# Two accumulating transfers behind a pair's q and k reads, and later starts for the heads of a gated linear attention, in a one-core encoder layer

## The chip, the cores and the metric

The kernel runs on one core of a Trainium2 chip and computes one layer of an encoder in one launch. The metric is the device time of one execution in microseconds; the time of a kernel is the median of its timed runs. Lower is better.

The core has a matmul engine (PE, whose weight loads the profile lists apart as PEld), a vector engine (DVE), a scalar engine (ACT), a general engine (POOL) and a queue engine (SP). PE reads the on-chip memory SBUF and writes eight banks of the accumulator memory PSUM, each 128 partitions by 512 float32. SP and POOL start the transfers (DMA) that carry data between the large off-chip memory and SBUF; POOL can also start a transfer that adds what it carries to what lies at its destination.

## What is computed

The layer normalizes x (512 rows of 2048), projects it once with a wide matrix, gives half of the projected columns to an attention with three dilations and the other half to a gated linear attention, joins both, projects back, and ends with a gated feed-forward block. Cut to what matters here:

```python
def reference(x, ...):
    h = rmsnorm(x, attn_norm_w[l])
    proj = h @ w_in[l]
    aq, ak, av, gq, gk, gv, gr, glr = jnp.split(proj, split_idx, axis=-1)
    attn = mixture_of_dilations(_heads(aq, 16), _heads(ak, 16), _heads(av, 16), rel_bias_table)
    ...
    # gated linear attention, 4 heads, both directions
    fwd = gla_causal(qh, kh, vh, log_a_f)
    bwd = flip(gla_causal(flip(qh), flip(kh), flip(vh), flip(log_a_b)))
    o = fwd + bwd
    o = o * lax.rsqrt(jnp.mean(o * o, axis=-1, keepdims=True) + NORM_EPS)
    gla_out = (_merge_heads(o) * gla_norm_w[l]) * jax.nn.silu(gr)
    mixed = jnp.concatenate([attn_out, gla_out], axis=-1) @ w_out[l]
    x = x + mixed
    h = rmsnorm(x, ffn_norm_w[l])
    x = x + (silu(h @ w_gate[l]) * (h @ w_up[l])) @ w_down[l]
    return rmsnorm(x, final_norm_w)
```

## The kernel before

**Products.** Every float32 operand is split into a high part and a low part of PE's rounded float32 type, and a product is three matmuls: high by high, high by low, low by high. ACT makes the high part (a cast) and DVE the low part (the difference). The matmuls of the plain projections are L346, L347 and L348. One such matmul starts 0.23 us after the one before; I call these the job matmuls.

**Order of the work.** The program is written as Python generators. A main line runs through the projections (jobs) and between two products lets side work go one step on: `run_side` takes a step of the generators in `side` (attention, linear attention), and `urgent` holds generators that go first. What an engine executes is fixed by the order in which these steps emit instructions; each engine works its own list in order, and an instruction that waits holds up all that stand behind it on that engine.

**The last unit of the front.** `Front.run` computes 16 units of the projection with seven products in place of eight (a Strassen-like scheme). Unit u leaves its result in a buffer `c_` by `evac7`: ACT and DVE combine seven PSUM banks, and then POOL starts four accumulating transfers (L1640 to L1643) that add three more buffers (r1, r2, r3) to `c_`. `finish` multiplies `c_` by the rows' scale (DVE, L1743) and POOL writes it to off-chip memory (L1744); for units 8 to 15 the destination is `qkd`, the attention's q and k. Of the last unit, u = 15, the multiplication and the write are kept back in `fr.late`, which `before_first` calls at step 8 of the next job (the projection of gv).

**Reads of a pair.** Attention works on pairs of heads. `read_qk` starts eight POOL reads for each pair (L574, 128 KB each, `a<-qkd`), and `load_qk` turns them into operands: four ACT instructions (L598) and four DVE instructions (L594). ACT L704 and DVE L710 make the high and low part of an attention unit's transposed weights; PE L696 is the transpose ahead of them.

**POOL's transfers.** A transfer that POOL starts reports its end on one of eight semaphores, taken in turn (in the rows below DMASW0 to DMASW7). A POOL transfer waits until the one that stands eight transfers ahead of it has landed.

**Linear attention.** `gla(h)` is a generator for one head, some 25 steps long. In its order: two PSUM banks z with the gate's projection (PE L977); ACT and DVE turn them into running sums and exponentials (`centre`, `exps`, `times`); then, for each direction d, a bank `tr` with transposes of k (PE L1071) and a bank `a` with k times q (PE L1074), which DVE copies under a mask into a zeroed buffer T (L1077) while ACT copies `tr`; then sums over blocks (PE L1096), states and outputs, the norm, and at the end two banks of transposes (PE L1166) that DVE scales and gates (L1169). `heads` then makes high and low parts of the result (ACT L963, DVE L956), which the output projection uses as stationary or moving operand. T is zeroed by POOL (L1066), and for every second head POOL also starts the reads of v (L906).

`turns` runs the four heads staggered: it lets at most two heads go on by one step each in a round, and starts a new head every `APART` = 12 rounds. PSUM banks are handed out from a list of free ones, the one that has been free longest first, so the order in which the steps ask decides which bank a step gets, and whose release it must wait for.

Of the kernel before, what the change touches and what calls it, by code (L numbers as in the profile page):

```python
# [29 lines left out]
NG = 4  # L30
# [82 lines left out]
def put(*slots):  # L113
    for s in slots:
        if s.home is not None:
            s.home.free.append(s.i)


def layer(nc, tc, x, attn_norm_w, w_in, rel_table, gw_f, gb_f, gw_b, gb_b, gla_norm_w, w_out,
# [7 lines left out]
    with tc.manual_schedule(), \  # L127
# [677 lines left out]
                yield  # L805
            urgent.append(last_pair(NH // 2 - 1))

        def turns(todo, apart):

            now, n = deque(), 0  # L810
            while todo or now:
                if n % apart == 0 and todo:
                    now.append(todo.popleft())
                for _ in range(2):
                    if _ < len(now):
                        g = now[0]
                        now.rotate(-1)
                        if next(g, 0) == 0:
                            now.remove(g)
                            continue  # L820
                    yield
                n += 1
# [85 lines left out]
        def evac_gv(pr):  # L908
            def f(banks):
                for t in range(4):  # L910
                    if t % 2 == 0:
                        v = s4.get(F32, [P, 2, 512])
                    if t % 2:
                        dve.tensor_scalar(v.t[:, 1], banks[t].t, rstd1[:, t:t + 1], None, op0=OP.mult)
                    else:
                        act.activation(v.t[:, 0], banks[t].t, AF.Copy, scale=rstd1[:, t:t + 1])
                    put(banks[t])
                    if t % 2:
                        pool.dma_start(out=gvd[2 * pr + t // 2], in_=v.t.rearrange("p b c -> p (b c)"))
                        put(v)  # L920
                if pr == 0:
                    side.append(silus())
                    side.append(turns(deque(gla(h) for h in range(NG)), APART))
            return f

        grd = dr.tile([4, P, 1024], F32, name="grd")
# [40 lines left out]
        def gla(h):  # L967
# [82 lines left out]
            exps(1)  # L1050
            yield
            times(1)
            if h % 2 == 0:
                load_gv(h // 2)
            yield
# [4 lines left out]
            if h == NG - 1:  # L1060
                put(*G["res"])

            T, kt = [], []
            for d in range(2):
                T.append(s2.get())
                pool.memset(T[d].t, 0.0)  # L1066
            for d in range(2):
                tr, a = ps.get(), ps.get()
                for b in range(4):
# [203 lines left out]
        def before_first(i):  # L1273
            if i == 1:
                urgent.appendleft(load_qk(0))
            if i == 4:
                load_v(0)
            if i == 8:
                fr.late()

        n_front = len(jobs)
        RATES = (4.5, 4.0)
        APART = 12
        for pr in range(2):
            j = job("B", [piece512(w_in, C_GV + pr * 512, k) for k in range(0, KT, 2)], list(range(KT)), acts_h,
                    evac_gv(pr), rate=RATES[0], start=None if pr else gstart, limit=3,
# [222 lines left out]

        class Feed(Blocks):  # L1510

# [96 lines left out]
            def evac7(self, u, banks):  # L1611


                a, z = slice(0, 256), slice(256, 512)
                add = lambda o, x_, y_: dve.tensor_tensor(o, x_, y_, op=OP.add)  # L1615
                sub = lambda o, x_, y_: dve.tensor_tensor(o, x_, y_, op=OP.subtract)
                c_ = s4.get(F32, [P, 2, 512])
                c = c_.t.rearrange("p f t -> p (f t)")
                m1, t2, t1, t3, m2, t4, b22 = (b.t for b in banks)
                t, v, r1, r2, r3 = (s2.get() for _ in range(5))  # L1620
                act.copy(t.t[:, a], m1[:, a])
                act.copy(r3.t[:, a], t1[:, z])
                act.copy(r2.t[:, z], t1[:, z])
                act.copy(r3.t[:, z], t3[:, z])
                act.copy(r1.t[:, a], m2[:, z])
                act.copy(c[:, 512:768], t4[:, a])
                act.copy(r2.t[:, a], t4[:, z])
                act.copy(c[:, 256:512], b22[:, a])
                act.copy(r1.t[:, z], b22[:, z])
                add(t.t[:, a], t.t[:, a], m1[:, z])  # L1630
                sub(t.t[:, z], t.t[:, a], t2[:, a])
                sub(t.t[:, z], t.t[:, z], t2[:, z])
                add(v.t[:, a], t1[:, a], t.t[:, z])
                add(v.t[:, z], t3[:, a], t.t[:, z])
                add(c[:, 768:1024], t1[:, a], v.t[:, z])
                add(c[:, a], m2[:, a], t.t[:, a])
                put(*banks)
                yield
                add(c[:, 256:768], c[:, 256:768], v.t)
                pool.dma_start(out=c[:, 0:512], in_=r1.t, accum_op=OP.add)  # L1640
                pool.dma_start(out=c[:, 512:1024], in_=r2.t, accum_op=OP.add)
                pool.dma_start(out=c[:, 256:768], in_=r3.t, accum_op=OP.add)
                pool.dma_start(out=c[:, 768:1024], in_=r3.t[:, z], accum_op=OP.add)  # L1643
                put(r1, r3, t, r2, v)
                for _ in range(3 if u < len(self.units) - 2 else 7):
                    yield
                yield from self.finish(u, c_, c)
# [73 lines left out]

        class Front(Feed):


            def __init__(self):
                self.units = [(w_in, C_GR + g * 256) for g in range(4)] + [(w_in, C_GQ), (w_in, C_GK)] + \
# [26 lines left out]
            def run(self):  # L1753
                banks = {}
                for i, (u, q) in enumerate(self.seq):
                    banks.setdefault(u, [])
                    self.load()
                    self.split(i)
                    self.sums(i + 1)
                    self.sums(i + 2)  # L1760
                    self.split(i + 1)
                    if u == len(self.units) - 1 and q < 3:
                        st.until, st.limit = in_pieces, q + 1
                        st.load()
                    while 2 * q + 1 not in xi:
                        run_side(1)
                    if u == len(self.units) - 1 and q == 3:
                        st.split(jobs[n_front].first + 2)
                    self.products(i, banks[u])
                    if u == len(self.units) - 1:  # L1770
                        for p in (2 * q, 2 * q + 1):
                            put(*xi.pop(p)["slots"])
                        if q == 1:
                            for _ in read_qk(0):
                                pass
                        if q == 2:
                            gla_operands()
                    done = None
                    if q == self.per - 1:
                        if u == len(self.units) - 1:  # L1780
                            s2.free.rotate(14)
                        done = self.evac7(u, banks.pop(u))
                        next(done)
                        if u == len(self.units) - 1:
                            next(done)
                    run_urgent()
                    if done:
                        urgent.append(done)

        fr = Front()  # L1790
# [469 lines left out]
```

## Time and profile before

| | us |
|---|---|
| median of 3 timed runs | 2164.08 (2163.97 to 2167.96) |
| the profiled execution, its own time | 2162.85 |
| span of the profiled execution | 2161.1 |
| PE busy in it | 2145.8 |
| DVE busy | 1851.8 |
| ACT busy | 1226.6 |
| POOL busy | 381.9 |

PE is busy in all but 15.3 us of the span. The time outside the span (2162.85 less 2161.1) is 1.75 us. In the profile a row of the timeline gives the start, the duration, the engine, the line, the operation, output and inputs by their names in the program, and in brackets how long the engine had been idle and what ended that. Matmuls overlap: one lasts about 0.4 us while the next starts after 0.23 us, so a loss on PE is read from start to start.

### The profile page before, as it was taken

The numbers are of one execution on the slowest core, as the hardware profiler recorded it, in microseconds if no ns is written. First come the engines' busy times: TensorE is split into PE (matmuls) and PEld (weight loads), VectorE is DVE, ScalarE is ACT, GpSimd is POOL, SyncE is SP. The second block draws the span as 40 slices with busy tenths as digits, with TensorE's granted clock in tenths as the row PEclk, the third lists the DMA queues.
The fourth block names the chain that finished last, engine by engine and source line by source line (L and its number), as shares of the span: only waits on it lengthen the run. The fifth ranks groups of instructions, "written<-read, shape, count | busy, mean of one in ns | idle before, by whom it ended". The sixth has DMA issues, their size and how long they took to land.

```text
span 2161.1 us, 35266 instructions
## 1 busy us (share of the span) xinstructions
PE 2145.8 (99%) x12754; PEld 1896.5 (88%) x12754; DVE 1851.8 (86%) x3153; ACT 1226.6 (57%) x2236; POOL 381.9 (18%) x531
## 2 busy tenths in 40 slices
PE   9999999999999999999999999999999999999998
PEld 7888888888888889888888888888888899999987
DVE  5699999878877778899899998998989888888795
ACT  7455555478876446455555555555555655555462
POOL 0011222232222010021122121221122120021300
PEclk9999999999999999999999999999999999999999
DMA  6377777877586763567677667776776985576982
GB/s 203 124 186 184 182 178 185 198 215 219 176 244 196 254 235 100 153 173 185 179 178 197 172 185 187 180 185 176 185 191 173 265 211 177 178 183 155 281 310 78
DMA packets 268220, 411.53 MB, mean 190 GB/s; under 512 B 19725, under 2 KB 164349, under 8 KB 268046
## 3 DMA queue, kind: packets, MB, share of 16 engines
q1 hardware_dynamic: 206110, 274.59, 40.1%
q0 software_dynamic: 61616, 134.15, 28.4%
q8 instruction: 101, 1.65, 0.3%
q14 instruction: 73, 0.60, 0.1%
q10 hardware_dynamic: 320, 0.53, 0.1%
HBM read 289.57 MB, written 66.42 MB: 165 GB/s over the span
## 4 chain that ended last, share of the span: by engine, by line
PE 90%; DVE 4%; DMA 4%; ACT 1%; issue 1%; POOL 0%; DVEq 0%; SPq 0%; ACTq 0%; POOLq 0%
PE ps L1595 31%; PE ps L1581 16%; PE ps L346 6%; PE ps L347 6%; PE ps L348 6%; PE ps L1962 5%; PE ps L1961 5%; PE ps L1960 5%; DMA b<-a 3%; PE ps L696 1%; DVE b L1504 1%; DMA a<-qkd 1%; PE ps L2155 1%; PE ps L2157 1%; PE ps L2156 1%
## 5 line engine op out<-in xcount | busy, mean ns | idle before, releaser
L1499 ACT CAST b<-b 128x1024 fp32r<-128x1024 f32 (+1 forms) x601 | 549.0, 944 | 405.6 <-DVE b L1504 209.7
L1504 DVE TENSOR_TENSOR b<-b,b 128x1024 fp32r<-128x1024 f32 (+1 forms) x601 | 630.6, 1084 | 31.7 <-ACT b L1499 20.2
L1595 PE MATMUL ps<-b,b 128*128 128x512 f32 x1760 | 517.2, 393 | 0.4 <-ACT b L1499 0.2
L1595 PE MATMUL ps<-a,b 128*128 128x512 f32 x1488 | 436.4, 393 | 0.2 <-DVE b L1615 0.2
L1595 PEld LDWEIGHTS ps<-b,b 128*128 128x128 f32 x1760 | 298.1, 188 | 33.2 <-ACT b L1499 0.7
L1581 PEld LDWEIGHTS ps<-b,b 128*128 128x128 f32 x1760 | 289.8, 190 | 42.6 <-DVE b L1504 0.3
L1581 PE MATMUL ps<-b,b 128*128 128x256 f32 x1760 | 318.1, 280 | 0.0
L1581 PEld LDWEIGHTS ps<-a,b 128*128 128x128 f32 x1488 | 246.5, 189 | 39.9 <-DVE b L1504 1.2
L1595 PEld LDWEIGHTS ps<-a,b 128*128 128x128 f32 x1488 | 248.9, 188 | 25.3 <-issue 0.4
L1581 PE MATMUL ps<-a,b 128*128 128x256 f32 x1488 | 267.6, 281 | 0.4 <-DVE b L1504 0.4
L1486 DVE TENSOR_TENSOR b<-b 128x512 f32<-128x512 f32 x276 | 189.2, 685 | 22.3 <-PE ps L1962 12.2
L1960 PE MATMUL ps<-b,b 128*128 128x256 f32 x624 | 176.6, 283 | 0.0
L1961 PE MATMUL ps<-b,b 128*128 128x256 f32 x624 | 176.6, 283 | 0.0
L1962 PE MATMUL ps<-b,b 128*128 128x256 f32 x624 | 176.6, 283 | 0.0
L346 PE MATMUL ps<-b,b 128*128 128x512 f32 x336 | 136.5, 406 | 0.2 <-DVE b L477 0.2
L348 PE MATMUL ps<-b,b 128*128 128x512 f32 x336 | 131.9, 392 | 0.0
L347 PE MATMUL ps<-b,b 128*128 128x512 f32 x336 | 131.8, 392 | 0.0
L1488 DVE TENSOR_TENSOR b<-b,b 128x256 f32<-128x256 f32 x276 | 117.5, 426 | 9.5
L1487 DVE TENSOR_TENSOR b<-b,b 128x256 f32<-128x256 f32 x276 | 117.3, 425 | 9.6
L1640 POOL DMA_DIRECT2D b<-a x58 | 50.2, 866 | 414.9 <-ACT b L1499 266.5
L1960 PEld LDWEIGHTS ps<-b,b 128*128 128x128 f32 x624 | 119.8, 192 | 0.0
L1961 PEld LDWEIGHTS ps<-b,b 128*128 128x128 f32 x624 | 119.8, 192 | 0.0
(296 smaller groups left out, 3972.8 us busy)
## 6 DMA issues: line engine op xcount, KB each, us to landing
b<-in_w_gate_dram SPq DMA_DIRECT2D x109, 512.0 KB, 4.0
b<-in_w_in_dram SPq DMA_DIRECT2D x94, 512.0 KB, 4.0
b<-in_w_up_dram SPq DMA_DIRECT2D x88, 512.0 KB, 4.2
b<-in_w_down_dram SPq DMA_DIRECT2D x88, 512.0 KB, 5.2
b<-a POOLq DMA_DIRECT2D x174, 256.0 KB, 4.6
b<-in_w_out_dram SPq DMA_DIRECT2D x32, 512.0 KB, 5.7
gd<-b POOLq DMA_DIRECT2D x22, 512.0 KB, 3.9
b<-gd SPq DMA_DIRECT2D x22, 512.0 KB, 7.7
```

Source lines behind the costliest of these rows:

```text
L346: mm(o, xh.t[:, c], wh.t[:, w], start=first and not on, stop=False, skip_group_check=on)
L347: mm(o, xh.t[:, c], wl.t[:, w], start=False, stop=False, skip_group_check=on)
L348: mm(o, xl.t[:, c], wh.t[:, w], start=False, stop=last, skip_group_check=on)
L1486: dve.tensor_tensor(s_[:, :, 0:2], r[:, :, 1:3], r[:, :, 0:1].to_broadcast(shape), op=OP.add)
L1488: dve.tensor_tensor(s_[:, :, 3], s_[:, :, 2], r[:, :, 3], op=OP.add)
L1499: act.copy(o, src)
L1504: dve.tensor_tensor(o, src, h, op=OP.subtract)
L1581: mm(o, wl, xh, start=False, stop=end, skip_group_check=True)
L1595: mm(o.rearrange("p (s t) -> p s t", s=2), wh, x_, start=first and p == 0, stop=False, skip_group_check=True)
L1960: mm(o, xh[:, t], wh, start=first and h == 0, stop=False, skip_group_check=True)
L1961: mm(o, xh[:, t], wl, start=False, stop=False, skip_group_check=True)
L1962: mm(o, xl[:, t], wh, start=False, stop=last, skip_group_check=True)
```

## The change

Three things are changed.

The last unit of the front is `parted`: after the first two accumulating transfers its generator stops, and the second two (L1642, L1643; in the new file L1651, L1652) are started by `before_first` at step 6 of the gv job. What is left of the generator is kept in `fr.rest`, not in `urgent`. Buffers t and v are given back before the stop.

`turns` starts the heads at rounds 0, 13, 25 and 37, in place of 0, 12, 24 and 36.

The two T buffers of a head are taken and zeroed two steps earlier, ahead of the reads of v.

```diff
-        def turns(todo, apart):
+        def turns(todo, starts):
 
             now, n = deque(), 0
             while todo or now:
-                if n % apart == 0 and todo:
+                if n in starts and todo:
                     now.append(todo.popleft())
...
             times(1)
+            T = [s2.get() for _ in range(2)]
+            for d in range(2):
+                pool.memset(T[d].t, 0.0)
             if h % 2 == 0:
                 load_gv(h // 2)
             yield
...
-            T, kt = [], []
-            for d in range(2):
-                T.append(s2.get())
-                pool.memset(T[d].t, 0.0)
+            kt = []
...
             if i == 4:
                 load_v(0)
+            if i == 6:
+                next(fr.rest)
             if i == 8:
+                for _ in fr.rest:
+                    pass
                 fr.late()
...
-        APART = 12
+        STARTS = (0, 13, 25, 37)
...
         class Feed(Blocks):
+            parted = False
...
                 pool.dma_start(out=c[:, 0:512], in_=r1.t, accum_op=OP.add)
                 pool.dma_start(out=c[:, 512:1024], in_=r2.t, accum_op=OP.add)
+                if self.parted and u == len(self.units) - 1:
+                    put(t, v)
+                    yield
+                    t = v = None
                 pool.dma_start(out=c[:, 256:768], in_=r3.t, accum_op=OP.add)
                 pool.dma_start(out=c[:, 768:1024], in_=r3.t[:, z], accum_op=OP.add)
-                put(r1, r3, t, r2, v)
+                put(*(o for o in (r1, r3, t, r2, v) if o))
...
         class Front(Feed):
+            parted = True
...
                     run_urgent()
-                    if done:
+                    if done and u == len(self.units) - 1:
+                        self.rest = done
+                    elif done:
                         urgent.append(done)
```

On POOL, at the end of the front, the rows before were these. `b_499` is the last unit's `c_`, `b_478` that of the unit before; the reads into `a_` are the second pair's, and the names in brackets are the semaphores that a row waits for (DMASW0 to 7 are the eight of POOL's own transfers, DMAHW those of transfers that SP starts).

```order
L1640 DMA b_499_4315<-a_142_4318 128x512 [waits DMASW3_49,DVE_49,Activation_49]
L1641 DMA b_499_4315<-a_143_4319 128x512 [waits DMASW4_49]
L1642 DMA b_499_4315<-a_144_4320 128x512 [waits DMASW5_49,DMASW4_49,DMASW3_49]
L1643 DMA b_499_4315<-a_144_4320 128x256 [waits DMASW6_49]
L1744 DMA qkd<-b_478_4107 128x1024 [waits DMASW7_49,DVE_49]
L574 DMA a_160_4466<-qkd 64x512 [waits DMASW0_49]
L574 DMA a_160_4466<-qkd 64x512 [waits DMASW1_49]
L574 DMA a_162_4468<-qkd 64x512 [waits DMASW2_49,PE_49]
L574 DMA a_162_4468<-qkd 64x512
L574 DMA a_161_4467<-qkd 64x512 [waits DMAHW0_49]
L574 DMA a_161_4467<-qkd 64x512 [waits DMASW5_49]
L574 DMA a_163_4469<-qkd 64x512 [waits DMASW6_49,PE_49]
```

The rows now:

```order
L1645 DMA b_499_4315<-a_142_4318 128x512 [waits DMASW3_49,DVE_49,Activation_49]
L1646 DMA b_499_4315<-a_143_4319 128x512 [waits DMASW4_49]
L1754 DMA qkd<-b_478_4107 128x1024 [waits DMASW5_49,DVE_49]
L574 DMA a_158_4463<-qkd 64x512 [waits DMASW6_49]
L574 DMA a_158_4463<-qkd 64x512 [waits DMASW7_49]
L574 DMA a_160_4465<-qkd 64x512 [waits DMASW0_49]
L574 DMA a_160_4465<-qkd 64x512 [waits DMASW1_49]
L574 DMA a_159_4464<-qkd 64x512 [waits DMASW2_49]
L574 DMA a_159_4464<-qkd 64x512 [waits DMASW3_49]
L574 DMA a_161_4466<-qkd 64x512 [waits DMAHW0_49,DMASW4_49]
L574 DMA a_161_4466<-qkd 64x512 [waits DMASW5_49]
L1651 DMA b_499_4315<-a_144_4320 128x512 [waits DMASW6_49]
```

The write of `b_478` and the eight reads now stand right behind the first two accumulating transfers. The old L1642 waits for both of these to land (DMASW3 and DMASW4), since it adds to the same buffer; now the sixth read waits for DMASW3 and the seventh for DMASW4, and the second two accumulating transfers come after the eighth.

On PE, where the first head of the linear attention makes its banks `tr` (L1071) and `a` (L1074) and the second head its two banks z (L977), the rows before were these; the digit behind `ps` is the PSUM bank, and the other rows are job matmuls.

```order
L1071 MATMUL ps1_324_6866<-idn_71,a28_381_6770 128x128 x4
L1074 MATMUL ps3_325_6867<-a13_380_6769,a28_381_6770 128x128 x4
L346 MATMUL ps6_321_6743<-b9_643_6686,b27_590_5987 128x512
L347 MATMUL ps6_321_6743<-b9_643_6686,b27_590_5987 128x512
L348 MATMUL ps6_321_6743<-b9_643_6686,b27_590_5987 128x512
L977 MATMUL ps2_326_6883<-a9_157_4452,a14_358_6372 128x512
L977 MATMUL ps4_327_6885<-a9_157_4452,a2_362_6436 128x512
L346 MATMUL ps7_322_6744<-b9_643_6686,b27_590_5987 128x512
L347 MATMUL ps7_322_6744<-b9_643_6686,b27_590_5987 128x512
L348 MATMUL ps7_322_6744<-b9_643_6686,b27_590_5987 128x512
L1071 MATMUL ps3_328_6893<-idn_71,a32_385_6803 128x128 x4
L1074 MATMUL ps1_329_6894<-a17_384_6802,a32_385_6803 128x128 x4
```

The same place now, from behind the first two rows, which are as before (`tr` of the first direction in bank 1, `a` in bank 3):

```order
L346 MATMUL ps7_322_6743<-b9_644_6685,b27_591_5986 128x512
L347 MATMUL ps7_322_6743<-b9_644_6685,b27_591_5986 128x512
L348 MATMUL ps7_322_6743<-b9_644_6685,b27_591_5986 128x512
L1071 MATMUL ps2_326_6884<-idn_71,a10_383_6802 128x128 x4
L1074 MATMUL ps4_327_6885<-a32_382_6801,a10_383_6802 128x128 x4
L346 MATMUL ps0_323_6744<-b9_644_6685,b27_591_5986 128x512
L347 MATMUL ps0_323_6744<-b9_644_6685,b27_591_5986 128x512
L348 MATMUL ps0_323_6744<-b9_644_6685,b27_591_5986 128x512
L977 MATMUL ps3_328_6902<-a9_157_4450,a15_356_6371 128x512
L977 MATMUL ps1_329_6904<-a9_157_4450,a2_360_6435 128x512
```

Before, the second direction's `tr` took bank 3, which the first direction's `a` had held. Now it takes bank 2 and its `a` bank 4, and the second head's z take banks 3 and 1, six job matmuls later than before.

At the end of the last head, on DVE, the rows before were these; `b29` and `b2` are the operands that `heads` makes (L956), and L1555 and L218 are other work of the weights to come and of the output projection.

```order
L1169 SCALAR_TENSOR_TENSOR a10_482_7915<-ps6_384_7910,wcol_74,b30_605_6240 128x512
L1169 SCALAR_TENSOR_TENSOR a18_483_7922<-ps4_385_7917,wcol_74,b30_605_6240 128x512
L1555 TENSOR_TENSOR b19_715_7850<-b19_715_7850 128x2x128 x2
L218 TENSOR_TENSOR a33_481_7901<-b24_709_7765,a20_480_7900 128x512
L1555 TENSOR_TENSOR b22_716_7890<-b22_716_7890 128x2x128
L956 TENSOR_TENSOR b29_720_7939<-a10_482_7915,b29_720_7939 128x512
L1555 TENSOR_TENSOR b22_716_7890<-b22_716_7890 128x2x128
L956 TENSOR_TENSOR b2_722_7949<-a18_483_7922,b2_722_7949 128x512
```

And now (L1560 is the old L1555):

```order
L1169 SCALAR_TENSOR_TENSOR a12_478_7921<-ps5_384_7916,wcol_74,b12_606_6239 128x512
L1169 SCALAR_TENSOR_TENSOR a2_479_7928<-ps6_385_7923,wcol_74,b12_606_6239 128x512
L218 TENSOR_TENSOR a14_477_7899<-b24_710_7754,a29_476_7898 128x512
L1560 TENSOR_TENSOR b11_718_7880<-b11_718_7880 128x2x128 x3
L956 TENSOR_TENSOR b23_723_7948<-a12_478_7921,b23_723_7948 128x512
L218 TENSOR_TENSOR a10_481_7932<-b24_710_7754,a32_480_7931 128x512
L956 TENSOR_TENSOR b19_724_7955<-a2_479_7928,b19_724_7955 128x512
```

About as much DVE work stands between L1169 and L956 as before, while on PE 12 job matmuls now stand between L1166 and the first use of the result, where 18 stood.

More of the change, by code (lines that the diff above doesn't have):

```diff
@@ L922, in f @@
                     side.append(silus())
-                    side.append(turns(deque(gla(h) for h in range(NG)), APART))
+                    side.append(turns(deque(gla(h) for h in range(NG)), STARTS))
             return f
```

## The prediction, made before the changed kernel had run

> **What bounds the kernel now.** I read the page's busy times first.
>
> ```profile
> span 2161.1 us, 35266 instructions
> PE 2145.8 (99%) x12754; PEld 1896.5 (88%) x12754; DVE 1851.8 (86%) x3153; ACT 1226.6 (57%) x2236; POOL 381.9 (18%) x531
> ```
>
> PE sets the end: 15.3 us of the span are not PE's. The change removes no matmul, so it can win only where PE stands idle. The view of busy time by windows says where that is (start and end, length, PE busy with its count, granted clock, DMA share, GB/s):
>
> ```profile
> 430.00:460.00 30.00, 28.49 (x145) 1.00 0.84 257
> 460.00:610.00 150.00, 149.10 (x878) 1.00 0.64 193
> 635.00:660.00 25.00, 23.42 (x117) 1.00 0.71 222
> 660.00:700.00 40.00, 39.75 (x202) 1.00 0.67 212
> ```
>
> Most of the rest lies in the kernel's last stage, which no edit touches. The edits reach 430 to 460 (1.51 us idle), 460 to 610 (0.90), 635 to 660 (1.58) and 660 to 700 (0.25): 4.24 us in all is the most that could go. The view of PE's waits names the two large ones (who waits <- for whom: us, times, longest):
>
> ```profile
> PE ps L1071 <- DVE a L1077: 1.6, 1, 1.6
> PE ps L696 <- DVE b L710: 1.5, 1, 1.5
> ```
>
> Each is one wait. They are the two places that the change aims at.
>
> **The first stall, at 447.55.** The chain of waits followed back from it (start, duration, what):
>
> ```profile
> 424.32 11.39 DMA b<-a
> ...
> 438.42 8.43 DMA a<-qkd
> ...
> 448.59 0.70 DVE b L710
> ```
>
> POOL stood before L1642 (its row below) until the second accumulating transfer (L1641, started at 424.32) had landed at 435.71; behind it stood the write of the unit before and all eight reads of the second pair. The first two reads landed at 446.85, ACT's L598 had waited for them, and L704 and L710 behind it, which end at 449.29, were what PE waited for. The timelines of POOL, ACT and PE give the sizes:
>
> ```profile
> 436.23 0.86 POOL L1642 DMA_DIRECT2D b<-a  x1 [11.03 <-DMA b<-a]
> 437.87 3.27 POOL L574 DMA_DIRECT2D a<-qkd  x5
> 446.93 0.63 ACT L598 ACTIVATE a<-a 128x512 fp32r<-128x512 f32 x1 [4.11 <-DMA a<-qkd]
> 450.87 0.62 ACT L598 ACTIVATE a<-a 128x512 fp32r<-128x512 f32 x1
> 447.31 0.40 PE L347 MATMUL ps<-a,b 128*128 128x512 f32 x1
> 447.55 0.39 PE L348 MATMUL ps<-a,b 128*128 128x512 f32 x1
> 449.43 0.63 PE L696 MATMUL ps<-idn,a 128*128 128x128 f32 x4 [1.49 <-DVE b L710]
> ```
>
> The matmul step is 447.55 less 447.31, so about 0.23 (0.24 here). PE would have gone on at 447.78 and did at 449.43: **1.65 us lost**. ACT was free 4.11 us before 446.93, at 442.82, so the reads had to land about there to be free, and at 445.2 or so for PE to lose nothing.
>
> With the change L1642 and L1643 stand behind the reads. The write and the first reads need nothing that is late: POOL's next issue can follow L1641 at once. With this queue's spacing (5 reads in 3.27) the write starts near 426 and the first two reads at 427 to 428, ten us ahead of the 437.87 of before. The sixth to eighth read still wait, for L1640 and L1641 to land, so until 435.7 again. But these feed the third and fourth L598, and the third began at 450.87 before; a landing of 8.43 behind 435.7 is 444.1 plus the spacing of three issues, about 446. So nothing is late on ACT, and the stall's 1.65 us go. The landing of such a read takes
>
> ```profile
> a<-qkd POOLq DMA_DIRECT2D x21, 128.0 KB, 8.2
> ```
>
> (count, size, median us to landing, of 400 to 460). Even 10 us behind 428 is 438, before 442.82. I take 1.65 of gain; from none (the reads late for another reason) to 1.65.
>
> The transfers now at the back, L1651 and L1652, lead to the late multiplication of the last unit:
>
> ```profile
> 464.30 1.23 DVE L1743 TENSOR_TENSOR b<-b,a 128x1024 f32<-128x1024 f32 x1
> ```
>
> Started with the eighth read near 437, they have 27 us; nothing is late there. The DMA engines move the same bytes. On this I cost the move at nothing, hidden by those 27 us.
>
> The Trainium skill, page "DMA: Bandwidth & Descriptors", section "Queues, rings and completion order", says that descriptors of a ring are consumed in order on each SDMA engine, and that a semaphore's increment lands only after every earlier write of that SDMA engine. That speaks against the change: the reads, though issued at 427, would report only after L1640's and L1641's own data, which landed at 435.7 by the chain above. By it the first reads would come at 436 or a little later, which is still ahead of 442.82, and the sum would be the same; if the full 8.43 came on top, it would be 444.1, and part of the margin to 445.2 would be left. It bears on the first rival.
>
> **The second stall, at 639.70.** PE and DVE there:
>
> ```profile
> 636.75 0.60 PE L1071 MATMUL ps<-idn,a 128*128 128x128 f32 x4
> 638.76 0.63 PE L977 MATMUL ps<-a,a 96*128 96x512 f32 x2
> 639.70 0.40 PE L348 MATMUL ps<-b,b 128*128 128x512 f32 x1
> 641.68 0.66 PE L1071 MATMUL ps<-idn,a 128*128 128x128 f32 x4 [1.58 <-DVE a L1077]
> 640.90 0.72 DVE L1077 COPY_PREDICATED a<-masks,ps 128x512 f32<-128x512 uint32 x1
> 645.82 1.46 PE L1096 MATMUL ps<-b,a 128*128 128x256 f32 x6
> ```
>
> The second direction's `tr` asked for the bank of the first one's `a`, and had to wait until DVE, which was busy without a gap up to 640.90, had copied it. From 639.70 plus 0.23 to 641.68 PE lost **1.75 us**. Now this `tr` has bank 2, which is free. Bank 3 goes to the second head's first z instead. The two z (L977) took 0.48 before (638.76 to 639.70, less two steps of 0.23) and no longer stand ahead, so the new L1071 starts at 639.93 less 0.48, or 639.45; from an L1071 to the L977 behind it and three job matmuls were 2.01 (636.75 to 638.76), so PE reaches the z at 641.46. The copy L1077 ends at 641.62. A wait of 0.1 to 0.2 can be left; I take 1.6 of gain, from none to 1.75. It is one head of four: the other heads start where the banks stand otherwise, and their waits are the 0.25 of the window 660 to 700. I take 0.2 of that.
>
> **The T buffers.** The memsets now go ahead of the reads of v, which so start later by their time:
>
> ```profile
> 631.98 1.50 POOL L906 DMA_DIRECT2D b<-gvd  x2
> 636.46 1.01 POOL L1066 MEMSET a<- 128x512 f32 x2
> 660.59 1.31 POOL L1066 MEMSET a<- 128x512 f32 x2
> DMA to landing us min/median/max: 5.9/8.4/10.4
> ```
>
> With 1.31 the reads of v start at 633.3 and land, at the longest 10.4, at 643.7. Their first reader, L1096, starts at 645.82 before, and 1.75 earlier now, at 644.1. That covers it, by 0.4 us at worst: nothing. Without that cover the price is what 10.4 is exceeded by. The memsets were before in nobody's way (L1077 at 640.90 is the first to need T), so their move wins nothing either.
>
> **The last head's end.** Here the shift costs. Its transposes L1166 stand six job matmuls (1.39) later, and their result is used at the same place in the output projection:
>
> ```profile
> 749.05 1.04 PE L1166 MATMUL ps<-idn,b 128*128 128x128 f32 x8
> 749.69 1.41 DVE L1169 SCALAR_TENSOR_TENSOR a<-ps,wcol,b 128x512 f32<-128x512 f32 x2 [3.11 <-PE ps L1166]
> 751.01 0.87 DVE L1555 TENSOR_TENSOR b<-b 128x256 f32<-128x256 f32 x2
> 751.81 0.68 DVE L218 TENSOR_TENSOR a<-b,a 128x512 fp32r<-128x512 f32 x1
> 752.74 0.68 DVE L956 TENSOR_TENSOR b<-a,b 128x512 fp32r<-128x512 f32 x1
> 754.50 0.39 PE L348 MATMUL ps<-a,b 128*128 128x512 f32 x1
> ```
>
> On the clock of before, L1166 now starts at 750.44 and L1169 at 751.08. Behind it come two L1169 (749.69 to 751.01: 1.32), one L218 and a block (751.81 to 752.74: 0.93), a pair of blocks (751.01 to 751.81: 0.80), and L956: it starts at 754.13 and ends at 754.81. The low part that it makes is first read by the L348 that was at 754.50 (the two matmuls before it read the high part, ACT's). That is **0.31 us of new wait**, with the hand-over from DVE to PE (449.29 to 449.43 above: 0.14) 0.45; bounds nothing (DVE may be a little quicker, as it stood idle 3.11 before) and 0.85, one more block of 0.40 in front of it. I take 0.45.
>
> **The sum.** −1.65 −1.6 −0.2 +0.45 = −3.0 us of PE's idle time. Span 2161.1 − 3.0 = 2158.1; with the same 1.75 around it the profiled execution is 2159.85 (before 2162.85). The median of the runs before is 2164.08, 1.23 above its profiled execution, so the same shift gives 2161.1. I forecast 2161.0.
>
> **Rivals.**
> (a) Late reads. The first reads of the second pair still land at 446 or later, because the DMA engines are full (share 0.84 in the window from 430) or because of the ring's order; the place is the same L598. Then the first 1.65 are not won: 2162.7. For it: landings there have a median of 8.2. Against: the reads start ten us earlier and have 15 us for 8.43.
> (b) The bank wait only moves. The second head's z wait as long as `tr` did (DVE is just as busy, the copy ends at 641.6, and the z's end frees the next bank), or L1096 waits for v. Then 1.6 is not won: 2162.6. Against: six more job matmuls are in front.
> (c) Slower. At the last head's end DVE meets an L1560 whose weights have not landed: L1560 stands ahead of L956 in DVE's list, while before a block already landed stood there. The price is a landing of a weight load, or one with the next behind it:
>
> ```profile
> 752.47 3.26 SPq L1467 DMA_DIRECT2D b<-in_w_gate_dram  x2
> b<-in_w_gate_dram SPq DMA_DIRECT2D x109, 512.0 KB, 4.0
> ```
>
> 4.0, or 4.0 and 3.26, is 2165 to 2168.4. It decides once the wait exceeds the 3.0 won. Against: before, the blocks ran there without a wait, and the loads are two pieces ahead.
> (d) More than summed: all 4.24 of the windows go, or the median of the new kernel lies as near to its profiled execution as could be: 2159.7 or less. Against: 0.90 of it lies in many small waits of attention, which nothing here addresses.
>
> The Trainium skill, page "GPSIMD Engine Reference", section "1. Specifications", says that POOL shares its SBUF interfaces with VectorE and collides with its instructions that read two SBUF inputs. The moved memsets now fall beside such instructions; the same two memsets took 1.01 in one row above and 1.31 in another, which fits it. By it the reads of v would be 1.31 late rather than 1.01, and of (b) the wait of L1096 for v would hang on the 0.4 us left.
>
> **How the numbers follow.** The forecast 0.53, (a) 0.13, (b) 0.12, (c) 0.10, (d) 0.12. About 0.2%, 4.3 us, is what a measurement of this kernel can tell from no change: faster is below 2159.8, slower above 2168.4. The forecast's own range, with the bounds of its terms and a median up to 1.2 off, is 2159.3 to 2162.4. Faster is (d) and a fifth of the forecast: 0.23. Slower is part of (c), where more than one load is late: 0.07. The rest, 0.70, is no change that can be told. For 8 in 10 the range takes in (a) and (b) and most of (d) and leaves out the upper part of (c): 2158.8 to 2164.4.
>
> **What would show it.** In the profile after: PE's waits without L696 <- L710 and L1071 <- L1077; POOL's first reads of the second pair before 430, and the sixth behind a wait for `b<-a` that ends near 435.7; L598 of that pair starting at about 442.8; window 430 to 460 with 0.2 or less idle. A short wait of L977 on L1077, up to 0.2, and a wait of L348 on L956 of 0.4 to 0.5 near 751. Wrong would be: L598 still idle for a read at 445; a wait of L1096 on `b<-gvd`; DVE idle before L1560 on a weight load; PE's total idle at 13 us or more (12.3 forecast).

## The result, and the profile after

| | before | changed |
|---|---|---|
| median, us | 2164.01 (6 runs, 2163.73 to 2167.96) | 2156.76 (6 runs, 2155.62 to 2157.88) |
| ratio of the runs | 1 | 0.9964, 95% interval 0.9951 to 0.9977 |
| profiled execution, own time | 2162.85 | 2156.72 |
| its span | 2161.1 | 2154.9 |
| PE not busy in the span | 15.3 | 12.0 |

The changed kernel is 7.2 us faster, where 3.0 were forecast, and lies below the range. The page of the changed kernel:

```profile
span 2154.9 us, 35268 instructions
PE 2142.9 (99%) x12754; PEld 1896.3 (88%) x12754; DVE 1851.7 (86%) x3153; ACT 1226.0 (57%) x2236; POOL 382.3 (18%) x531
```

PE's busy time in the four windows that the edits reach (same columns as before):

```profile
430.00:460.00 30.00, 30.00 (x164) 1.00 0.83 224
460.00:610.00 150.00, 149.07 (x876) 1.00 0.67 202
635.00:660.00 25.00, 24.97 (x119) 1.00 0.75 242
660.00:700.00 40.00, 40.00 (x209) 1.00 0.73 234
```

Two of the windows are now without idle time, and one has 0.03. PE's idle time fell by 3.3 us, almost what was forecast (12.3 left, 12.0 found). But PE's *busy* time fell too, by 2.9, although it does the same 12754 matmuls. So most of what the forecast missed in this pair lies in time that the profile counts as busy. PE's waits after the change, between 410 and 770 (one more, L872 with 0.4, is the same in both profiles):

```profile
PE ps L696 <- ACT b L916: 0.6, 1, 0.6
PE ps L640 <- DVE b L710: 0.4, 1, 0.4
PE ps L348 <- DVE b L956: 0.3, 1, 0.3
```

Both large waits are gone, and the forecast one at the last head's end (L348 on L956) is there. The other two stand in the profile before as well, with 0.5 and 0.4.

To see where the time went, the starts of matmuls that do the same work were set beside each other in the two profiles (start before, start after, lead; each row's gain is its lead less the one above):

```
up to                                         before    after    lead   gain
the 31st matmul                                 9.98     8.47    1.51   1.51
ahead of the first stall                      443.29   441.59    1.70   0.19
behind it, with the units that follow         451.51   447.68    3.83   2.13
first L1071                                   636.75   632.78    3.97   0.14
first L1096, behind the second stall          645.82   640.34    5.48   1.51
last matmul                                  2152.43  2146.28    6.15   0.67
```

The first row is a surprise: at the kernel's very beginning, where nothing was edited, the changed kernel leads by 1.5 us. PE's timeline there, of before and then of the changed kernel:

```profile
6.39 0.76 PE L346 MATMUL ps<-b,b 128*128 128x512 f32 x1 [0.18 <-DVE b L477]
7.03 0.80 PE L347 MATMUL ps<-b,b 128*128 128x512 f32 x1
...
9.98 0.47 PE L348 MATMUL ps<-b,b 128*128 128x512 f32 x1
10.30 0.39 PE L346 MATMUL ps<-b,b 128*128 128x512 f32 x1
```

```profile
6.13 0.80 PE L346 MATMUL ps<-b,b 128*128 128x512 f32 x1
...
8.24 0.40 PE L347 MATMUL ps<-b,b 128*128 128x512 f32 x1
8.47 0.40 PE L348 MATMUL ps<-b,b 128*128 128x512 f32 x1
```

Before, one matmul still took 0.64 us to the next at 6.4, and the step of 0.23 came only at 10; in the changed kernel it was there at 8.2. Whether that belongs to the change was the first thing to test.

### The profile page after: what moved, and what is told of

It reads as the page before. It is cut to its first block, busy times and chain, and to the rows that moved or that the text cites. A ratio compares the mean times of both kernels' runs of the same rounds, so it can differ in the third digit from the quotient of the medians.

```text
span 2154.9 us, 35268 instructions
## 1 busy us (share of the span) xinstructions
PE 2142.9 (99%) x12754; PEld 1896.3 (88%) x12754; DVE 1851.7 (86%) x3153; ACT 1226.0 (57%) x2236; POOL 382.3 (18%) x531
## 3 DMA queue, kind: packets, MB, share of 16 engines
q8 instruction: 101, 1.65, 0.3%
## 4 chain that ended last, share of the span: by engine, by line
PE 97%; DVE 1%; DMA 0%; issue 0%; ACT 0%; DVEq 0%; POOL 0%; ACTq 0%
PE ps L1600 34%; PE ps L1586 17%; PE ps L348 7%; PE ps L346 7%; PE ps L347 7%; PE ps L1973 5%; PE ps L1974 5%; PE ps L1972 5%; PE ps L696 1%; PE ps L2169 1%; PE ps L2168 1%; PE ps L2167 1%; PE ps L721 1%; PE ps L720 1%; PE ps L640 1%; PE ps L641 1%
## 5 line engine op out<-in xcount | busy, mean ns | idle before, releaser
L348 PE MATMUL ps<-b,b 128*128 128x512 f32 x344 | 134.7, 392 | 0.0
```

The costliest lines, as they stand in the source:

```text
L348: mm(o, xl.t[:, c], wh.t[:, w], start=False, stop=last, skip_group_check=on)
```

## The experiments

Two theories stood at the start. **A**: the early lead varies between executions of one program, and the change's gain is that of its places; then the places must be worth more than the first profile shows. **B**: the lead comes with the changed program. Each kernel was timed in rounds beside the kernel before, e5 to e8 on a second chip; the kernel before scatters from 2158 to 2168 us over the two.

**e1, the kernel before again** (no edit).

> The kernel before, unchanged, timed against itself and profiled once more. It asks whether the 1.5 us by which the changed kernel led in its profile already at the first ten microseconds (granted clock full at 7.7 against 9.9 us), and the 1.1 us near 375 to 382, belong to the change or to a single execution. Theory A (they vary between executions of one program): the median is equal within 0.5 us, but the new profile reaches its 120th matmul, or its stretch near 375, at another time than the first profile, by 0.3 us or more. Theory B (the early lead comes with the changed program): the new profile repeats the old one within 0.2 us in both places.

2164.21 (2161.18 to 2167.98, 12 runs) against 2162.84 of the kernel before (31 runs), ratio 1.0006 (0.9997 to 1.0014): the same kernel's medians differ by 1.4 here, more than the 0.5 allowed. Its profile is what counts. Its 31st matmul starts at 8.39, not 9.98: 1.6 us earlier in the same program. So the early lead is a matter of the single execution. And the first stall is larger; PE's timeline of this execution:

```profile
445.08 0.39 PE L348 MATMUL ps<-a,b 128*128 128x512 f32 x1
448.31 0.63 PE L696 MATMUL ps<-idn,a 128*128 128x128 f32 x4 [2.84 <-DVE b L710]
```

It is the transpose that waited from 447.78 to 449.43 in the first profile. Here PE came 2.5 us earlier, at 445.31, and was let go only 1.1 us earlier: 3.00 us lost in place of 1.65. POOL explains why; its timeline in this execution:

```profile
424.48 1.05 POOL L1641 DMA_DIRECT2D b<-a  x1
436.57 0.86 POOL L1642 DMA_DIRECT2D b<-a  x1 [11.04 <-DMA b<-a]
```

These are 424.32 and 436.23 in the first profile. The accumulating transfers kept their time although PE was early; the 1.1 us come from the reads, which landed 7.0 to 7.8 us after their issue where the chain of the first profile has 8.43. The stall is not an amount that is lost; it ends at a time that the transfers set, and swallows what PE has won ahead of it.

**e2, the first part alone** (the transfers; heads every 12 rounds, T zeroed where it was).

```diff
-        STARTS = (0, 13, 25, 37)
+        STARTS = (0, 12, 24, 36)
...
-            T = [s2.get() for _ in range(2)]
-            for d in range(2):
-                pool.memset(T[d].t, 0.0)
             if h % 2 == 0:
                 load_gv(h // 2)
...
-            kt = []
+            T, kt = [], []
+            for d in range(2):
+                T.append(s2.get())
+                pool.memset(T[d].t, 0.0)
```

> The first part alone: the second two accumulating transfers behind the second pair's reads, with the heads started every 12 rounds and the T buffers zeroed where they were. Theory A (the sum of the places): the stall before L696 goes together with its echo, 2.1 us by the two profiles, nothing else: ratio about 0.9990, median near 2161.9. Theory B (the part of the gain that lies ahead of 410 us comes with this edit): 2.1 and 2.8 more, median near 2159.1, and the profile's early stretch as in the changed kernel. Rival that this edit does nothing alone: 2164.0.

2158.33 (2157.24 to 2159.78, 11 runs), ratio 0.9981 (0.9972 to 0.9989): 4.5 us, between the 2.1 of theory A and the 4.9 of theory B and nearer to B's; the scatter is 2.5 us where the kernel before has 7.1. But its early stretch is like e1's (31st matmul at 8.65), so the edit did not bring that. From ahead of the stall to behind it this profile wins 2.1 us on the first profile of before, but about 3.5 on that of e1. The early lead now goes through to the end.

**e3, the other two parts alone** (the last unit as before; heads at 0, 13, 25, 37, T zeroed early).

```diff
-            parted = True
+            parted = False
...
-            if i == 6:
-                next(fr.rest)
             if i == 8:
-                for _ in fr.rest:
-                    pass
                 fr.late()
...
```

> The other two parts together: heads started at 0, 13, 25, 37 and the T buffers zeroed before the reads of v, the last unit's transfers as before. Theory A: 1.4 us at the second L1071, 1.3 in small waits between 663 and 700, 0.2 elsewhere, 0.6 lost again at the last head's end: 2.3 net, median near 2161.7, stall before L696 still there with 1.5. Theory B (early gain with this edit): near 2158.9.

2161.16 (12 runs), ratio 0.9994 (0.9985 to 1.0002): 1.7 us, unclear beside the scatter, near the 2.3 of theory A. The stall is in its profile, again with 2.84.

**e4, the changed kernel again.**

> The changed kernel once more, on the same chip as the parts. Both theories: near 2156.8, 7.2 below the kernel before. Theory A: its new profile reaches its 120th matmul at another time than the first one by 0.3 us or more, and the lead over the parts is 2.1 and 2.3 as these give it. Theory B: the early stretch is as in its first profile within 0.2 us.

2156.94 (7 runs), ratio 0.9973 (0.9963 to 0.9984): 5.9 us on this chip, against 4.5 and 1.7 of the parts, which sum to 6.2. Its 31st matmul starts at 8.15, 0.3 earlier than in its first profile. Theory B falls.

**e5 and e6, 16 more matmuls ahead of the stall,** in the kernel before and in the changed one. If the stall ends at a time that the transfers set, work on PE ahead of it must be free.

```diff
+                            if first and b == 0 and j is jobs[n_front]:
+                                for _ in range(16):
+                                    mm(o, xh.t[:, c], wh.t[:, w], start=True, stop=True, skip_group_check=on)
                             mm(o, xh.t[:, c], wh.t[:, w], start=first and not on, stop=False, skip_group_check=on)
```

> The kernel before, with 16 more job matmuls on PE (3.7 us by the step of 0.23) at the first step of the gv job: the first high by high product of the first bank is done 16 times over, each overwriting the last. This lies behind the last unit's products and ahead of the stall before L696, so the chain of POOL transfers that ends the stall is not delayed. Theory A (the stall ends at the time that the transfers set, and swallows whatever PE brings ahead of it, 3.5 us in the profile of e1): PE's wait at L696 shrinks from 2.8 to nothing and 0.2 to 1 us are added: near 2164. Theory B (the stall is an amount of time that is lost as such, and the 1.5 of the first profile its usual size): 2.0 or more are added, and a wait of L696 of 1 us or more is left.

> The changed kernel with the same 16 matmuls in the same place. Theory A: nothing on PE waits for the transfers there, so all 3.7 us are added: 2160.6, and the changed kernel's lead over the one before shrinks to 2 to 4 us when both have them. Theory B: 3.7 added too, the lead stays at 6 to 7.

e5: 2162.5 (11 runs) against 2163.03, ratio 0.9996 (0.9987 to 1.0005). In the medians the 3.7 us cost nothing, even a little less than expected. e6: 2159.74 (11 runs), ratio 0.9988 (0.9979 to 0.9996), 2.8 above the 2156.94 of e4 where 3.7 were expected; so the same matmuls do cost in the changed kernel, and its lead shrinks to 2.8. In e5's profile PE no longer waits at that transpose (its line is L699 there):

```profile
447.96 0.39 PE L351 MATMUL ps<-a,b 128*128 128x512 f32 x1
448.19 0.60 PE L699 MATMUL ps<-idn,a 128*128 128x128 f32 x4
```

It starts one step of 0.23 behind the matmul ahead of it, at 448.19, where e1's started at 448.31 with 3.7 us less work done. In this execution the reads were early too (the first L598 starts at 444.21, in e1 at 445.82). Theory B, by which 2.0 or more would be added and a wait left, is out; what the medians owe to the swallowed work and what to the clock is told behind e9.

**e7, T zeroed where it was** (the rest as changed).

```diff
-            T = [s2.get() for _ in range(2)]
-            for d in range(2):
-                pool.memset(T[d].t, 0.0)
...
-            kt = []
+            T, kt = [], []
+            for d in range(2):
+                T.append(s2.get())
+                pool.memset(T[d].t, 0.0)
```

> The changed kernel with the T buffers zeroed where they were. If the earlier zeroing only takes POOL's time ahead of the reads of v, as the prediction has it, nothing changes: 2156.9, no new wait on L1077. If the zeroing has to be early because the copy L1077 now comes sooner after it, DVE waits for the memset, and PE behind it: 2157.5 to 2158.5 with a wait in the profile near 637 or at a later head.

2157.80 (8 runs, 2155.78 to 2158.08), ratio 0.9975 (0.9964 to 0.9985), not to be told from e4. Its profile has no wait on L1077, and its last matmul starts 0.35 us earlier than e4's, most of which it leads by already at 564. No worth of the zeroing shows, either way.

**e8, the last head at round 35.**

```diff
-        STARTS = (0, 13, 25, 37)
+        STARTS = (0, 13, 25, 35)
```

> The changed kernel with the last head of the linear attention started at round 35 in place of 37 (36 is not there for want of a free buffer). The wait of L348 on L956 at the last head's end, 0.6 us from start to start, should go: 2156.3. If the last head's own z or tr then meet a bank that DVE has not released, some or all of it comes back near 698 to 722: 2156.9 to 2158.

2158.78 (11 runs), ratio 0.9979 (0.9970 to 0.9988): the median is 1.8 above e4's, but the intervals overlap. The profile decides. The wait at the last head's end is gone, which wins 0.6 us on e4's profile, but another head's transposes now meet a bank that DVE holds (at 693.7), and between 657 and 702 it loses 1.6:

```profile
PE ps L1166 <- DVE a L1169: 0.8, 1, 0.8
```

**e9 and e10, the second two transfers earlier:** behind the write but ahead of all eight reads (step 2), and between the fourth and the fifth read (step 4).

```diff
-            if i == 6:
+            if i == 2:
                 next(fr.rest)
```

```diff
-            if i == 6:
+            if i == 4:
                 next(fr.rest)
```

> The changed kernel with the second two accumulating transfers started at step 2 of the gv job: the write of the unit before still goes ahead of them, but all eight reads of the second pair stand behind them again. If what counts is that the reads stand behind the wait for L1646 to land (some 436 us), the stall before L696 is back with 1.5 us or more, the median is near 2160.5 to 2161.5 (the parts of e3 kept) and the runs scatter over 6 us or more again, as those of the kernel before. If the write of the unit before, which the reads need, was what mattered, the stall is gone and the median near 2157.

> The same with the second two transfers at step 4: four reads ahead of them, four behind. Only the first two reads feed the first L598, the next two the second. If the stall hangs on these alone, the second half may land near 446 unharmed: 2157, no wait at L696. If the later reads were close as well (they land 12.5 us behind their issue in the changed kernel, so near 449 here, against a third L598 at 445.6 there), a stall of 2 to 4 us comes one or two transposes later: 2159 to 2161.

e9: 2161.45 (2159.12 to 2163.77, 11 runs), ratio 0.9991 (0.9982 to 1.0000). The stall is back, although the write of the unit before goes first; what counts is where the reads stand. PE's timeline:

```profile
449.04 0.63 PE L696 MATMUL ps<-idn,a 128*128 128x128 f32 x4 [3.37 <-DVE b L710]
```

The windows behind it (start and end, length, PE busy with its count, granted clock, DMA share, GB/s):

```profile
448.00:450.00 2.00, 0.96 (x6) 0.91 0.85 250
450.00:452.00 2.00, 2.00 (x10) 0.50 0.15 49
452.00:454.00 2.00, 2.00 (x11) 0.74 0.46 138
```

Behind the 3.37 us of idle PE ran at half clock, by these shares from about 449.6 to 453.0. From start to start PE loses 6.2 us between 440 and 470 in this execution, 5.7 in e3's, which has the same clock of 0.50, 4.5 in e1's, which has not, 3.1 in the first profile and 1.0 in the changed kernel's (each gap between matmuls less the usual one of its kind). The window from 450 to 452 in e3, then in e1:

```profile
450.00:452.00 2.00, 2.00 (x8) 0.50 0.07 25
450.00:452.00 2.00, 1.98 (x11) 1.00 0.19 59
```

How often does the clock fall? The mean granted clock of every timed run of e1 to e11, and of the changed kernel's first six, is on record, to three places. Half clock for 3.4 us lowers it by 0.0008: the two profiled executions that have it read 0.998, the eleven others 0.999. Of the 91 timed runs of the kernel before, 57 read less than 0.999; of e3's 12 runs eight do, of e9's 11 ten. Of the 78 runs of the kernels without the long wait at that transpose (the changed one, e2, e5 to e8, e10, e11), none does. The 57 have a median of 2164.2 us, the other 34 one of 2160.7. Where in a run the clock fell, the mean does not tell; only the two profiles do.

This changes the reading of e5. None of its 11 runs had the fall, but 18 of the 30 runs beside it did. Against the other 12, with a median of 2160.6, the 16 matmuls cost 1.9 of their 3.7 us. By this comparison the stall swallowed about half of them, and what they did cost was made up by the clock, which no longer fell. That the stall ends at the transfers' time stands; that work ahead of it is free is true of the medians alone.

e10: 2158.13 (8 runs), ratio 0.9974 (0.9964 to 0.9985). The first two L598 are in time, the third is late by its reads, and the small rest of a stall comes later, at L640. ACT's timeline, then PE's:

```profile
448.66 0.63 ACT L598 ACTIVATE a<-a 128x512 fp32r<-128x512 f32 x1 [3.04 <-DMA a<-qkd]
```

```profile
449.41 0.40 PE L348 MATMUL ps<-a,b 128*128 128x512 f32 x1
450.55 0.50 PE L640 MATMUL ps<-a,a 128*128 128x512 f32 x1 [0.74 <-DVE b L710]
```

From start to start that is 0.9 us (450.55 less 449.41 less 0.23), less than the 2 to 4 expected, so the third L598 seems to have been needed later than I had taken it. The medians do not tell e10 from e4 (ratios 0.9974 and 0.9973); by this 0.9 us of the profile, all eight reads have to stand ahead.

**e11, one empty step less ahead of the last head's transposes,** the rest as changed.

```diff
             put(*os_)
             yield
-            yield
+            if h < NG - 1:
+                yield
```

> The changed kernel with one of the two empty steps ahead of the transposes L1166 left out for the last head, so that these come six job matmuls (1.4 us) sooner after ACT's scaling. The wait of L348 on L956, 0.6 us, should go: 2156.3. If L1166 then meets ACT's scaling unfinished, PE waits there in its place: 2156.6 to 2157.5.

2156.01 (5 runs, 2154.95 to 2156.13), ratio 0.9963 (0.9951 to 0.9976). The interval overlaps that of e4 by far, so the clock does not separate the two; the profile has no wait on L956 any more, and set beside e4's it wins 0.65 us between 744 and 750, of which 0.5 are left at its last matmul. By that half microsecond it is the best version found.

## Why the prediction was wrong in size and right in place

**The failed step is the size of the first stall**: "1.65 us lost", with 1.65 as the upper bound. The mechanism was read right (L1642's wait for L1641 ahead of the reads) and goes with the edit, but 1.65 is the loss in one execution, whose PE was late at the stall: by 2.5 us against e1, of which 1.6 come from its first ten microseconds. Between 440 and 470 the first profile loses 2.1 more than the changed one; in e1, e3 and e9 the loss there is 3.5 to 5.2 above the changed kernel's 1.0 (3.0 to 3.5 for the stall, a little more behind it and, in two of three, the half clock). The first part alone gave 4.5 in the medians. The prediction had a hint: the profiled execution was 1.23 below the median, which it carried over to the changed kernel as it stood. There the two are 0.04 apart.

The Trainium skill, page "TensorE: Matmul & The Clock Gate", section "Part 1: The HAM clock gate (the "warmup" mystery)", says that PE falls to half rate after an idle window of about 3.4 us, that the window runs free, and that the number of slow matmuls at a start differs from run to run. The rows agree in part: half clock came behind gaps of 3.37 (e9) and 2.84 (e3), the second of them well short of that window, and none came behind the 2.84 of e1 or the 1.49 of the first profile; the end of the slow start moved by 1.5 us between the two profiles of the pair. The prediction did not ask what an idle time near that length costs behind it.

**The cap of 4.24 us failed with it.** It was PE's idle time in four windows. A matmul is shown as busy for 0.4 us where the next could start after 0.23, so a short wait hides in it. In the window 660 to 700 before, which shows 0.25 idle, these are the rows:

```profile
666.47 0.66 PE L1071 MATMUL ps<-idn,a 128*128 128x128 f32 x4
667.20 1.16 PE L1074 MATMUL ps<-a,a 128*128 128x128 f32 x8
...
697.56 1.03 PE L977 MATMUL ps<-a,a 96*128 96x512 f32 x2
698.42 0.40 PE L346 MATMUL ps<-b,a 128*128 128x512 f32 x1
698.67 0.40 PE L347 MATMUL ps<-b,a 128*128 128x512 f32 x1
698.90 0.40 PE L348 MATMUL ps<-b,a 128*128 128x512 f32 x1
699.34 0.66 PE L1071 MATMUL ps<-idn,a 128*128 128x128 f32 x4
```

From L1071 to L1074 it is 0.73, where it was 0.43 at the first head (636.75 to 637.18); the two z take 0.86 where they took 0.47; and L1071 waits 0.21 beyond the step. Over the window such losses sum to 1.15 from start to start, of which the changed kernel keeps 0.1 to 0.2. "I take 0.2" should have been about 1.

**The reads**: right in that they wait, and lucky in time. POOL's timeline of the changed kernel, the time to landing of its reads issued up to 428.4, and ACT's timeline:

```profile
426.04 0.55 POOL L574 DMA_DIRECT2D a<-qkd  x1
...
433.01 0.52 POOL L574 DMA_DIRECT2D a<-qkd  x1 [1.92 <-DMA b<-a]
435.33 0.52 POOL L574 DMA_DIRECT2D a<-qkd  x1 [1.81 <-DMA b<-a]
437.70 0.52 POOL L574 DMA_DIRECT2D a<-qkd  x1 [1.85 <-DMA qkd<-b]
```

```profile
DMA to landing us min/median/max: 12.5/12.8/13.1
```

```profile
441.08 0.62 ACT L598 ACTIVATE a<-a 128x512 fp32r<-128x512 f32 x1
```

The sixth and seventh read wait for the two accumulating transfers and the eighth for the write, as the order of the semaphores has it; the prediction had put the eighth behind the accumulating transfers too, at 435.7, and it starts at 437.70. And the first reads land 12.5 to 13.1 us after their issue, at 439 to 440 against the 438 worked out with ten, and L598 needs them at 441.08: about 1 us to spare, not five. In e4 it waited 0.17 for them. That they report only after the two transfers and the write ahead of them (the waits for these end by 437.70) is what the Trainium skill's rule on ring order, cited in the prediction, would have; by it the prediction put the first reads between 436 and 444.1. No run tests whether the rule is the reason.

**The second stall**: right. The gain there is 1.51 against the 1.6 forecast, and the short wait that should be left is there; PE's rows of the changed kernel, and DVE's:

```profile
637.28 0.40 PE L348 MATMUL ps<-b,b 128*128 128x512 f32 x1
637.71 0.73 PE L977 MATMUL ps<-a,a 96*128 96x512 f32 x2
```

```profile
636.93 0.73 DVE L1077 COPY_PREDICATED a<-masks,ps 128x512 f32<-128x512 uint32 x1
```

637.71 is 0.20 behind the step, just after the copy's end at 637.66.

**The last head's end**: right, a little larger, 0.61 against 0.45. DVE's timeline of the changed kernel, then PE's:

```profile
747.54 0.69 DVE L956 TENSOR_TENSOR b<-a,b 128x512 fp32r<-128x512 f32 x1
```

```profile
747.55 0.39 PE L347 MATMUL ps<-a,b 128*128 128x512 f32 x1
748.28 0.50 PE L348 MATMUL ps<-a,b 128*128 128x512 f32 x1 [0.34 <-DVE b L956]
```

748.28 is 0.50 behind the step, and 0.11 more are lost behind it. **The T buffers**: no worth shows, as said (e7). But the prediction's two memset rows do not fit what it cites of the Trainium skill: the shorter one (1.01, at 636.46) ran beside DVE instructions with two inputs, and for more than the first half of the longer one (1.31, at 660.59) DVE was idle, up to 661.33. In the changed kernel the moved pair, beside such instructions, took 1.67. **The rivals**: (a), (b) and (c) did not come; L1096 waits for no read, and no L1560 for a weight. (d) came: one of its ways, the median as near to its profiled execution as could be, makes 1.2 of the 4.2 us between forecast and measurement; the rest came by neither.

With the terms as measured in the pair of profiles, 2.1 + 1.5 + 1.3 − 0.6 is 4.3; the rest of the 6.2 is the early lead of 1.5, which belongs to the pair and not to the change, and some 0.3 in small pieces. In place of it, a usual execution of the kernel before loses another 1 to 3 us at the stall. By the count of clocks, most executions of the kernel before have the fall: the 34 runs without it lie 2.4 us above the median of e2, near the 2.1 of the pair, and the 57 with it 5.9. That the longer stall and the half clock behind it make up this difference is worked out from e1, e3 and e9; no run takes the two apart, and the six runs of the kernel before in the table of the result have no clock on record.

## What to carry to other kernels

A stall that ends when a transfer lands has no fixed size: it ends at the transfer's time and swallows whatever the waiting engine wins or loses ahead of it, so one profile gives one sample of it. Before it is priced, take a second profile, or add work ahead of it and see whether that is free, and compare the mean granted clock of many runs: here it told apart the runs whose clock had fallen, without a profile of each. And the idle time of an engine whose instructions overlap in the profile is no cap on what can be won there; read losses from start to start.

## What the runs showed of the hardware

A gap of about 3 us on PE can cost more than itself: after 2.84 us (e3) and 3.37 us (e9) of idle the granted clock was 0.50 between 450 and 452, for some 3.4 us in all, and with the same gap e3 lost 1.2 us more than e1 (5.7 against 4.5). After 2.84 us in e1 it stayed at 1.00. In the timed runs the mean clock was below 0.999 in 75 of 114 of the kernels whose profile has a long wait at that transpose (before, e3, e9) and in none of 78 of the others. The time at which PE reaches its full step at the start moved by 1.8 us between profiles (31st matmul at 8.15 to 9.98 us).
